# Opening of a hybrid attention and convolution layer: the first two blocks of products in another order, the first weight rows by two queues, two unread products fewer

## The chip, the cores and the metric

The kernel runs on one core of a Trainium2 chip. The metric is device time in microseconds (us) of one execution; lower is better. A core has five engines that run their own instruction lists side by side: TensorE (PE, matrix products; its weight loads are listed as PEld), VectorE (DVE), ScalarE (ACT), GpSimd (POOL) and SyncE (SP, which here only issues DMAs). They wait for one another by semaphores. DMAs are issued by SP, ACT and POOL.

## The reference, cut to what matters

One decoder layer on 512 tokens of width 2048:

```python
h = _rmsnorm(x, g_pre)
proj = h @ w_in                       # 2048 x 7168, all float32
q, k, v, z_att, u, g_glu, z_conv = jnp.split(proj, IN_SPLITS, axis=-1)
y_att  = stick_breaking_attention(q, k, v) * silu(z_att)
y_conv = conformer_conv(u, g_glu, ...) * silu(z_conv)   # starts with u * sigmoid(g_glu)
out = x + _rmsnorm(concat(y_att, y_conv) @ w_out, g_post)
```

The change touches only the start of `proj`: the first 512 columns of `g_glu`.

## The kernel before

Every float32 operand of a product is split into an upper part (`hi`, rounded to the format that PE takes) and a lower part (`lo`, the difference). A product of two such operands is three PE products that add up in one PSUM tile: upper by upper, upper by lower, lower by upper. One PE instruction multiplies a 128x128 tile by a 128x512 tile.

Nearly all of the kernel is a list of steps of such products, with the weights streamed in by DMA, split by ACT (`hi`) and DVE (`lo`), and used by PE. Ahead of the list stands the **opening**, which computes the first 512 columns of `g_glu` while `x` itself is still coming in. It works in 16 blocks: weight group `kg` of 0 to 3 (512 rows of `w_in`, tile `r_gn`, split into `h_gn` and `l_gn`) by token tile `m` of 0 to 3 (128 tokens). Four PSUM tiles `gn` (`ps0[m]`) collect the sums. The normalisation by the root of the mean square is multiplied in later, so the products can start on raw `x`.

For each block, `turn_block(n)` (L1255, by `turn_x`, L232) makes four 128x128 transposes of a tile of `x` on PE into a PSUM tile `xT`; then ACT writes the upper part into `h_hi` (L244) and DVE the lower part into `h_lo` (L245). For block 0 alone, DVE writes the upper part (L242) and, later, the lower part (`first_lo`, L247). `keep_raw` (L250) has ACT copy the raw transposed tile into `whole`. `rows_block` (L466) makes the products of a block: for each of four slices, `h_hi` by `h_gn` (L471) and `h_hi` by `l_gn` (L472), then four products of `h_lo` by `h_gn` (L478). The transposes of the next block are put in between: in block 0 after the third slice (`turn_at=2`), in the others after the first.

Group 0 of the weights comes as four tiles of 128 rows, 256 KB each (`load_w0_rows`, L1202), all issued by SP, between the first and the second tile of `x` (256 KB each as well). `part(0, i)` (L1211) splits row tile `i`: ACT writes `h_gn` (L102, multiplied by a column of `g_pre`), DVE `l_gn` (L103).

The order on PE, DVE and ACT in the opening is written out by hand, and each engine takes its instructions in the order of the program. Ahead of the first block, PE is kept at work by **unread products** (`idle_products`, L1242; tile `idle`): five before the transpose of `g_pre`, two after it, and four between the transposes of block 0 and its first product. Nobody reads their result. `plan` (L1271) hangs the rest of the work of ACT, DVE and the queues on the blocks: squares for the norm, splits of the next weights, further loads.

Of the kernel before, what the change touches and what calls it, by code (L numbers as in the profile page):

```python
# [16 lines left out]
P = 128  # L17
# [31 lines left out]
def hybrid_layer(  # L49
# [15 lines left out]
    nc = tc.nc  # L65
# [18 lines left out]
    def t2(name, dt=F32):  # L84
        return t2p.tile([P, S], dt, tag="t2", name=name)
# [4 lines left out]
    def mm(name):  # L90
        return mmp.tile([P, S], F32, tag="mm", name=name)

    def f32(ap):
        return ap.bitcast(F32)

    def split(hi, lo, src, scale=None):

        if scale is None:
            nc.scalar.activation(hi, src, AF.Copy)  # L99
            nc.vector.tensor_tensor(out=lo, in0=src, in1=f32(hi), op=ALU.subtract)  # L100
        else:
            nc.scalar.activation(hi, src, AF.Copy, scale=scale)  # L102
            nc.vector.scalar_tensor_tensor(  # L103
                out=lo, in0=src, scalar=scale, in1=f32(hi), op0=ALU.mult, op1=ALU.subtract
            )
# [123 lines left out]

    raw_h = {(m, 0): whole[:, :, m * P : (m + 1) * P] for m in range(NT)}  # L230

    def turn_x(m, j):  # L232

        ps = trp.tile([P, S], F32, tag="tr", name=f"xT{m}_{j}")
        for i in range(4):
            cs = slice(i * P, (i + 1) * P)
            nc.tensor.transpose(ps[:, cs], xts[m][j][:, cs], ident)
        src = ps.rearrange("p (i t) -> p i t", i=4)
        ms = slice(m * P, (m + 1) * P)
        hi, lo = h_hi[j][:, :, ms], h_lo[j][:, :, ms]  # L240
        if (m, j) == (0, 0):
            nc.vector.tensor_copy(hi, src)  # L242
        else:
            nc.scalar.activation(hi, src, AF.Copy)  # L244
            nc.vector.tensor_tensor(out=lo, in0=src, in1=f32(hi), op=ALU.subtract)  # L245

        def first_lo():  # L247
            nc.vector.tensor_tensor(out=lo, in0=src, in1=f32(hi), op=ALU.subtract)

        def keep_raw():  # L250
            if j > 0:
                raw_h[m, j] = t2(f"xw{m}_{j}").rearrange("p (i t) -> p i t", i=4)
            if (m, j) == (0, 0):
                first_lo()
            nc.scalar.copy(raw_h[m, j], src)

        return keep_raw
# [88 lines left out]
    def h_at(k, lo=0, hi=S):  # L346
        return h_hi[k // 4][:, k % 4, lo:hi], h_lo[k // 4][:, k % 4, lo:hi]
# [115 lines left out]
    def g_src(kg):  # L463
        return w_in[kg * S : (kg + 1) * S, C_G : C_G + S]

    def rows_block(kg, m, ps, w, between=(), turn_at=0):  # L466

        hi, lo = w
        parts = [h_at(kg * 4 + i, m * P, (m + 1) * P) for i in range(4)]
        for i, (a, _) in enumerate(parts):  # L470
            nc.tensor.matmul(ps, a, hi[:, i, :], start=kg + i == 0, stop=False, skip_group_check=True)  # L471
            nc.tensor.matmul(ps, a, lo[:, i, :], start=False, stop=False, skip_group_check=True)  # L472
            if i == turn_at:
                for f in between:
                    f()
        for i, (_, a) in enumerate(parts):
            last = kg == 3 and i == 3
            latest[0] = nc.tensor.matmul(  # L478
                ps, a, hi[:, i, :], start=False, stop=last, skip_group_check=True
            ).ins  # L480
# [33 lines left out]
    def sum_next(todo):  # L514

        if todo:
            tc.add_manual_dep(
                todo.popleft()().ins, latest[0].name,
                mybir.DependencyInfo(mybir.DependencyClass.Sync, mybir.DependencyReason.DATA),
                reason="not before its step",  # L520
            )
# [664 lines left out]
    ps0 = [mm(f"gn{m}") for m in range(NT)]  # L1186
    with tc.manual_schedule(engines={mybir.EngineType.DVE, mybir.EngineType.Activation}):
# [3 lines left out]
        w0 = {}  # L1191
# [10 lines left out]
        def load_w0_rows(i):  # L1202
            if 0 not in w0:
                w0[0] = (
                    raws.tile([P, 4, S], F32, tag="raw", name="r_gn0"),
                    his.tile([P, 4, S], F32R, tag="hi", name="h_gn0"),
                    los.tile([P, 4, S], F32R, tag="lo", name="l_gn0"),
                )
            nc.sync.dma_start(w0[0][0][:, i], g_src(0)[i * P : (i + 1) * P, :])

        def part(kg, i):  # L1211
            raw, hi, lo = w0[kg]
            k = kg * 4 + i
            split(hi[:, i], lo[:, i], raw[:, i], g_col[:, k : k + 1] if kg < 3 else None)
# [13 lines left out]
        for i in range(4):  # L1228
            load_w0_rows(i)
# [12 lines left out]
        def idle_products(count):  # L1242
            for i in range(count):
                nc.tensor.matmul(
                    idle.rearrange("p (n c) -> p n c", n=4), mean_w,
                    mean_w.unsqueeze(1).to_broadcast([P, 4, P]), start=True, stop=True,
                )
# [4 lines left out]
        blocks = [(kg, m) for kg in range(4) for m in range(NT)]  # L1252
        keeps = {}

        def turn_block(n):  # L1255
            kg, m = blocks[n]
            keeps[n] = turn_x(m, kg)
# [7 lines left out]
        def do(f, *args):  # L1265
            return partial(f, *args)
# [39 lines left out]
            15: [do(keep_rows, 2), do(next, first)],  # L1306
        }
        turn_block(0)
        idle_products(4)
        for i in range(4):  # L1310
            part(0, i)
        keeps[0]()
        for n, (kg, m) in enumerate(blocks):
            rows_block(
                kg, m, ps0[m], w0[kg][1:], [do(turn_block, n + 1)] if n + 1 < len(blocks) else (),
                2 if n == 0 else 0,
            )
            for f in plan[n]:
                f()
            if n + 1 < len(blocks):  # L1320
                keeps[n + 1]()
            if n >= 5 and n % 2:
                sum_next(v_sumq)
# [31 lines left out]
    for n, step in enumerate(steps):  # L1355
# [25 lines left out]
        w = loaded.pop(n)  # L1381
# [44 lines left out]
```

## Time and profile before

| | us |
|---|---|
| median of 3 runs | 860.49 |
| lowest to highest | 859.71 to 860.8 |
| profiled execution, device time | 860.66 |
| its span in the trace | 858.7 |
| PE busy in the span | 846.6 (99%) |

The span runs from the first to the last instruction that the trace shows; the remaining 1.96 us of the profiled execution lie around it. "Busy" of PE counts an instruction as busy from its start to its modelled end, waits of a product for its operand included; how fast PE moves is read from the distance between starts, which the chain of waits shows. In the chain, a row is a stretch that the next row had to wait for, or the instruction ahead of it on the same engine. Names in the rows leave out the buffer numbers: `gn` is any of the four PSUM tiles, `r_gn` any of the weight groups, `x` any of the 16 tiles of `x`.

### The profile page before, as it was taken

The page shows a single profiled execution, that of the slowest core. Times are in us where ns is not written, and L with a number is a line of the kernel's source. Part 1 is how long each engine was busy: PE and PEld are TensorE (multiplying, and loading weights), DVE is VectorE, ACT ScalarE, POOL GpSimd, SP SyncE. Part 2 cuts the span into 40 slices and gives each one's busy share as a digit, 9 for nine tenths or more (in the row PEclk, how much of TensorE's full clock was granted, in tenths as well). Part 3 has the DMA queues.
Part 4 walks back from the last instruction along what each step waited for, and adds up shares of the span by engine and source line. Part 5 has one row for each costly group of instructions (what it writes and reads, how often), then busy time and mean ns, then how long its engine had stood idle before and what let it go on. Part 6 is the DMA issues. An engine that isn't in the chain of part 4 may idle for free.

```text
span 858.7 us, 9932 instructions
## 1 busy us (share of the span) xinstructions
PE 846.6 (99%) x3868; PEld 701.9 (82%) x3868; DVE 660.7 (77%) x795; ACT 416.3 (48%) x473; POOL 139.4 (16%) x170
## 2 busy tenths in 40 slices
PE   9999999999999999999999999999999999999995
PEld 6888888788888888888888888888888888888884
DVE  5798899767579798897969898368964776468775
ACT  6784222555444342436432535369844355455542
POOL 0111110010130224222031334330000100000031
PEclk9999999999999999999999999999999999999999
DMA  8698989475877879867689887937755995557783
GB/s 322 236 291 186 326 262 248 151 239 196 295 224 227 244 147 207 283 181 208 190 221 187 239 244 152 289 103 289 295 196 196 222 267 196 197 197 269 281 279 100
DMA packets 92134, 195.04 MB, mean 227 GB/s; under 512 B 3686, under 2 KB 45938, under 8 KB 86712
## 3 DMA queue, kind: packets, MB, share of 16 engines
q1 hardware_dynamic: 66400, 120.61, 40.9%
q0 software_dynamic: 22304, 69.21, 33.8%
q10 hardware_dynamic: 3384, 4.59, 1.5%
q8 instruction: 30, 0.49, 0.2%
q14 instruction: 16, 0.13, 0.0%
HBM read 186.01 MB, written 75.50 MB: 305 GB/s over the span
## 4 chain that ended last, share of the span: by engine, by line
PE 84%; DVE 8%; DMA 4%; ACT 2%; issue 1%; POOL 0%; DVEq 0%; ACTq 0%; POOLq 0%
PE za L343 3%; PE za L342 3%; PE za L344 3%; PE a L1067 3%; PE a L1065 3%; PE a L1066 3%; PE u L344 3%; PE u L343 3%; PE u L342 3%; DVE acc L401 3%; PE q L344 3%; PE k L344 3%; PE q L342 3%; PE k L343 3%; PE k L342 3%; PE q L343 3%
## 5 line engine op out<-in xcount | busy, mean ns | idle before, releaser
L401 DVE SCALAR_TENSOR_TENSOR acc<-hg,vec,acc 128x512 f32<-128x512 f32 x240 | 181.4, 756 | 7.3
L100 DVE TENSOR_TENSOR l_w<-r_w,h_w 128x2048 fp32r<-128x2048 f32 x28 | 64.1, 2291 | 42.6 <-ACT h_w L99 42.6
L99 ACT ACTIVATE h_w<-r_w 128x2048 fp32r<-128x2048 f32 x28 | 53.6, 1915 | 44.4 <-DMA r_w<-ws 14.7
L342 PE MATMUL u<-h_hi,h_u 128*128 128x512 f32 x128 | 50.1, 391 | 0.0
L342 PE MATMUL q<-h_hi,h_q 128*128 128x512 f32 x128 | 50.1, 391 | 0.0
L342 PE MATMUL za<-h_hi,h_za 128*128 128x512 f32 x128 | 50.0, 391 | 0.0
L342 PE MATMUL k<-h_hi,h_k 128*128 128x512 f32 x128 | 50.0, 391 | 0.0
L344 PE MATMUL k<-h_hi,l_k 128*128 128x512 f32 x128 | 49.9, 390 | 0.0
L344 PE MATMUL u<-h_hi,l_u 128*128 128x512 f32 x128 | 49.9, 390 | 0.0
L344 PE MATMUL za<-h_hi,l_za 128*128 128x512 f32 x128 | 49.9, 390 | 0.0
L344 PE MATMUL q<-h_hi,l_q 128*128 128x512 f32 x128 | 49.9, 390 | 0.0
L343 PE MATMUL u<-h_lo,h_u 128*128 128x512 f32 x128 | 49.8, 389 | 0.0
L343 PE MATMUL k<-h_lo,h_k 128*128 128x512 f32 x128 | 49.8, 389 | 0.0
L343 PE MATMUL za<-h_lo,h_za 128*128 128x512 f32 x128 | 49.8, 389 | 0.0
L343 PE MATMUL q<-h_lo,h_q 128*128 128x512 f32 x128 | 49.8, 389 | 0.0
L1065 PE MATMUL a<-h_w,f_hi 128*128 128x512 f32 x128 | 49.8, 389 | 0.0
L1066 PE MATMUL a<-l_w,f_hi 128*128 128x512 f32 x128 | 49.8, 389 | 0.0
L1067 PE MATMUL a<-h_w,f_lo 128*128 128x512 f32 x128 | 49.8, 389 | 0.0
L100 DVE TENSOR_TENSOR l_v<-r_v,h_v 128x2048 fp32r<-128x2048 f32 x14 | 32.0, 2289 | 17.0 <-ACT h_v L99 17.0
L100 DVE TENSOR_TENSOR l_z<-r_z,h_z 128x2048 fp32r<-128x2048 f32 x14 | 32.0, 2288 | 16.2 <-ACT h_z L99 16.2
L674 POOL TENSOR_SCALAR_AFFINE_SELECT t<-t 128x128 f32<-128x128 f32 x64 | 35.2, 585 | 53.6 <-ACT t L710 29.5
L99 ACT ACTIVATE h_v<-r_v 128x2048 fp32r<-128x2048 f32 x14 | 26.8, 1916 | 29.4 <-PE g L343 13.2
(370 smaller groups left out, 2239.5 us busy)
## 6 DMA issues: line engine op xcount, KB each, us to landing
ws<-in_w_out_dram POOLq DMA_DIRECT2D x24, 1024.0 KB, 9.4
r_w<-ws SPq DMA_DIRECT2D x16, 1024.0 KB
vs<-in_w_in_dram POOLq DMA_DIRECT2D x12, 1024.0 KB, 11.8
zs<-in_w_in_dram POOLq DMA_DIRECT2D x12, 1024.0 KB, 9.4
r_w<-in_w_out_dram SPq DMA_DIRECT2D x12, 1024.0 KB
r_u<-in_w_in_dram SPq DMA_DIRECT2D x8, 1024.0 KB
r_q<-in_w_in_dram SPq DMA_DIRECT2D x8, 1024.0 KB
r_k<-in_w_in_dram SPq DMA_DIRECT2D x8, 1024.0 KB
```

The source lines that it names most:

```text
L99: nc.scalar.activation(hi, src, AF.Copy)
L100: nc.vector.tensor_tensor(out=lo, in0=src, in1=f32(hi), op=ALU.subtract)
L342: nc.tensor.matmul(ps, wh, ah, start=first, stop=False)
L343: nc.tensor.matmul(ps, wh, al, start=False, stop=False)
L344: latest[0] = nc.tensor.matmul(ps, wl, ah, start=False, stop=last).ins
L401: bgq.append(lambda j=j: nc.vector.scalar_tensor_tensor(out=acc, in0=hg[:, j : j + S], scalar=vec[:, ct, j : j + 1], in1=acc, op0=ALU.mult ...
L674: nc.gpsimd.affine_select(out=blk, in_=blk, compare_op=ALU.is_gt, fill=0.0, base=0, pattern=[[-1, P]], channel_multiplier=1,)
L1065: nc.tensor.matmul(ps, fh[:, kk, ts], hi[:, k, :], start=st, stop=False, skip_group_check=True)
L1066: nc.tensor.matmul(ps, fh[:, kk, ts], lo[:, k, :], start=False, stop=False, skip_group_check=True)
L1067: nc.tensor.matmul(ps, fl[:, kk, ts], hi[:, k, :], start=False, stop=en, skip_group_check=True)
```

## The change

Four things change, all in the opening.

- Row tiles 0 and 2 of weight group 0 are issued by ACT's queue, row tiles 1 and 3 by SP's.
- Two of the four unread products between the transposes of block 0 and its first product are gone.
- Blocks 0 and 1 are taken apart. PE makes the products of the upper part of block 0 (the transposes of block 1 now stand after the second slice), those of block 1 (the transposes of block 2 after the third slice), and then the four products of the lower part of block 0 and the four of block 1. From block 2 on nothing changes.
- `first_lo` is called ahead of the blocks and no longer by `keep_raw`, and both raw copies (`keeps[0]`, `keeps[1]`) come after the upper products of both blocks. On ACT, the upper parts of blocks 1 and 2 thus come ahead of the raw copies of blocks 0 and 1.

```diff
+        if (m, j) == (0, 0):
+            lower_part.append(first_lo)
...
-            if (m, j) == (0, 0):
-                first_lo()
             nc.scalar.copy(raw_h[m, j], src)
...
-    def rows_block(kg, m, ps, w, between=(), turn_at=0):
+    def rows_block(kg, m, ps, w, between=(), turn_at=0, uppers=True, lowers=True):
...
-            nc.sync.dma_start(w0[0][0][:, i], g_src(0)[i * P : (i + 1) * P, :])
+            eng = nc.sync if i % 2 else nc.scalar
+            eng.dma_start(w0[0][0][:, i], g_src(0)[i * P : (i + 1) * P, :])
...
-        idle_products(4)
+        idle_products(2)
         for i in range(4):
             part(0, i)
+        lower_part[0]()
+
+        rows_block(0, 0, ps0[0], w0[0][1:], [do(turn_block, 1)], 1, lowers=False)
+        rows_block(0, 1, ps0[1], w0[0][1:], [do(turn_block, 2)], 2, lowers=False)
         keeps[0]()
+        keeps[1]()
         for n, (kg, m) in enumerate(blocks):
-            rows_block(
-                kg, m, ps0[m], w0[kg][1:], [do(turn_block, n + 1)] if n + 1 < len(blocks) else (),
-                2 if n == 0 else 0,
-            )
+            between = [do(turn_block, n + 1)] if 2 <= n < len(blocks) - 1 else ()
+            rows_block(kg, m, ps0[m], w0[kg][1:], between, uppers=n >= 2)
             for f in plan[n]:
                 f()
-            if n + 1 < len(blocks):
+            if 2 <= n + 1 < len(blocks):
                 keeps[n + 1]()
```

On PE, from the transposes of block 1 (`xT1`) on, the order before was this; `gn0` and `gn1` are the sums of blocks 0 and 1, `h_hi0` and `h_lo0` the parts of `x`, `h_gn0` and `l_gn0` those of the weights:

```order
L237 MATMUL xT1_0_212<-ident_91,x1_0_104 128x128 x4
L471 MATMUL gn0_139<-h_gn0_148,h_hi0_116 128x512
L472 MATMUL gn0_139<-l_gn0_149,h_hi0_116 128x512
L478 MATMUL gn0_139<-h_gn0_148,h_lo0_120 128x512 x4
L471 MATMUL gn1_140<-h_gn0_148,h_hi0_116 128x512
L472 MATMUL gn1_140<-l_gn0_149,h_hi0_116 128x512
L237 MATMUL xT2_0_228<-ident_91,x2_0_108 128x128 x4
```

On PE, from the last upper product of block 0 (its transposes `xT1` now stand two slices ahead of this point) to the last lower product of block 1, the order now is this:

```order
L476 MATMUL gn0_139<-l_gn0_149,h_hi0_116 128x512
L475 MATMUL gn1_140<-h_gn0_148,h_hi0_116 128x512
L476 MATMUL gn1_140<-l_gn0_149,h_hi0_116 128x512
...
L239 MATMUL xT2_0_224<-ident_91,x2_0_108 128x128 x4
L475 MATMUL gn1_140<-h_gn0_148,h_hi0_116 128x512
L476 MATMUL gn1_140<-l_gn0_149,h_hi0_116 128x512
L482 MATMUL gn0_139<-h_gn0_148,h_lo0_120 128x512 x4
L482 MATMUL gn1_140<-h_gn0_148,h_lo0_120 128x512 x4
```

The eight products of lower parts moved behind all upper products of both blocks, and the transposes of block 2 with them from the first slice of block 1 to its third.

On ACT, from the splits of the weight rows on, the order before was this:

```order
L102 ACTIVATE h_gn0_148<-r_gn0_147,g_col_125 128x512 x4
L255 COPY whole_131<-xT0_0_186 128x4x128
L244 ACTIVATE h_hi0_116<-xT1_0_212 128x4x128
L255 COPY whole_131<-xT1_0_212 128x4x128
L244 ACTIVATE h_hi0_116<-xT2_0_228 128x4x128
```

On ACT, from the issue of the two row tiles on, it now is this:

```order
L1214 DMA r_gn0_147<-in_w_in_dram 128x512 x2
L102 ACTIVATE h_gn0_148<-r_gn0_147,g_col_125 128x512 x4
L246 ACTIVATE h_hi0_116<-xT1_0_207 128x4x128
L246 ACTIVATE h_hi0_116<-xT2_0_224 128x4x128
L258 COPY whole_131<-xT0_0_186 128x4x128
L258 COPY whole_131<-xT1_0_207 128x4x128
```

The two upper parts moved ahead of the two raw copies, and two DMA issues are new. The order on DVE is what it was; SP has two issues fewer and is otherwise the same.

## Rows read from the trace of the kernel before

**Rows 1.** The head of the page, and its busy time by engine (us, share of the span, instructions).

```profile
span 858.7 us, 9932 instructions
PE 846.6 (99%) x3868; PEld 701.9 (82%) x3868; DVE 660.7 (77%) x795; ACT 416.3 (48%) x473; POOL 139.4 (16%) x170
```

**Rows 2.** The chain of waits in order of time, from the start to the first product of block 2: start us, us, what.

```profile
1.77 2.50 PE idle L1244 x5
...
5.63 0.99 PE xT L237 x4
6.62 1.65 PE idle L1244 x4
8.27 0.23 PE gn L471
...
8.95 0.28 PE gn L472
...
9.46 0.42 PE gn L472
9.88 0.44 PE xT L237 x4
...
10.55 0.23 PE gn L472
10.79 1.06 PE gn L478 x4
11.85 0.47 PE gn L471
...
12.55 0.44 PE xT L237 x4
...
14.38 0.93 PE gn L478 x4
15.31 0.23 PE gn L471
```

**Rows 3.** The timeline of DVE in the same stretch, looked at in narrow windows (start us, us, what, in brackets the idle time before and who ended it); rows of "x2" hold two splits that overlap, of which the first starts at the time shown.

```profile
6.66 0.69 DVE L242 CAST h_hi<-xT 128x512 fp32r<-128x512 f32 x1 [1.97 <-PE xT L237]
7.26 0.74 DVE L103 SCALAR_TENSOR_TENSOR l_gn<-r_gn,g_col,h_gn 128x512 fp32r<-128x512 f32 x1
7.92 1.41 DVE L103 SCALAR_TENSOR_TENSOR l_gn<-r_gn,g_col,h_gn 128x512 fp32r<-128x512 f32 x2
9.25 0.74 DVE L103 SCALAR_TENSOR_TENSOR l_gn<-r_gn,g_col,h_gn 128x512 fp32r<-128x512 f32 x1
9.91 0.68 DVE L248 TENSOR_TENSOR h_lo<-xT,h_hi 128x512 fp32r<-128x512 f32 x1
```

**Rows 4.** The timeline of ACT: the first split of a weight row, the third and fourth, the first raw copy, the upper part of block 1, and the first split of weight group 1.

```profile
6.18 0.72 ACT L102 ACTIVATE h_gn<-r_gn,g_col 128x512 fp32r<-128x512 f32 x1 [4.10 <-DMA r_gn<-in_w_in_dram]
7.45 1.36 ACT L102 ACTIVATE h_gn<-r_gn,g_col 128x512 fp32r<-128x512 f32 x2
10.68 0.59 ACT L255 COPY whole<-xT 128x512 f32<-128x512 f32 x1 [1.88 <-DVE h_lo L248]
11.16 0.60 ACT L244 ACTIVATE h_hi<-xT 128x512 fp32r<-128x512 f32 x1
16.98 1.34 ACT L102 ACTIVATE h_gn<-r_gn,g_col 128x512 fp32r<-128x512 f32 x2
```

**Rows 5.** The timeline of the loads: the first and the last row tile as SP issues them (start us, us of the issue), PE's first transposes, which wait for the first tile of `x`, and the load that SP issues once the second tile of `x` has landed.

```profile
1.23 0.42 SPq L1209 DMA_DIRECT2D r_gn<-in_w_in_dram  x1
2.76 0.43 SPq L1209 DMA_DIRECT2D r_gn<-in_w_in_dram  x1
5.50 0.71 PEld L237 LDWEIGHTS xT<-ident,x 128*128 128x128 f32 x4 [0.60 <-DMA x<-in_x_dram]
8.68 0.33 SPq L141 DMA_DIRECT2D x<-in_x_dram  x1
```

**Rows 6.** The table by stretches of time: from:to us, length, busy us of each engine, then PEclk (granted clock), mean share of the DMA engines, GB/s.

```profile
3.00:4.00 1.00, 1.00 (x3) 0.46 (x2) 0.00 (x0) 0.00 (x0) 0.00 (x0) 1.00 0.76 115
6.00:7.00 1.00, 1.00 (x5) 0.90 (x5) 0.34 (x1) 0.81 (x2) 0.00 (x0) 1.00 1.04 399
```

**Rows 7.** The view of the DMA queues (packets, MB, share of the 16 DMA engines): first SP's queue (q1) at 11 to 14 us, where it works alone, then ACT's queue (q10) and SP's at 80 to 88 us, where both and POOL's are at work.

```profile
q1 hardware_dynamic: 613, 1.18, 103.7%
...
q10 hardware_dynamic: 428, 0.78, 25.5%
q1 hardware_dynamic: 460, 0.45, 21.1%
```

**Rows 8.** The view of waits from 12 to 850 us, for PE (the one row of that answer) and for its weight loads (the three longest): who waited for whom, us in total, times, longest.

```profile
PE va L638 <- DVE l_v L100: 1.2, 1, 1.2
...
PEld va L638 <- DVE l_v L100: 1.6, 1, 1.6
PEld vb L638 <- DVE l_v L100: 0.9, 2, 0.5
PEld gn L471 <- ACT h_hi L244: 0.4, 1, 0.4
```

**Rows 9.** Rows of the chain of waits and of POOL's timeline after the opening: the transposes that release the norm, a copy of weights that POOL issues when PE has read a buffer, a load of weights, the split that waits for it, and the split at which PE's longest wait ends.

```profile
41.03 0.45 PE r_ps L273 x4
...
60.58 0.50 POOL L506 DMA_DIRECT2D vs<-vs  x1 [5.42 <-PE gn L478]
...
92.96 20.43 DMA r_k<-in_w_in_dram
113.50 1.93 ACT h_k L99
154.78 2.30 DVE l_v L100
```

More of the change, by code (lines that the diff above doesn't have):

```diff
@@ L230, in hybrid_layer @@
     raw_h = {(m, 0): whole[:, :, m * P : (m + 1) * P] for m in range(NT)}
+    lower_part = []
     def turn_x(m, j):
@@ L464, in g_src @@
         return w_in[kg * S : (kg + 1) * S, C_G : C_G + S]
-    def rows_block(kg, m, ps, w, between=(), turn_at=0):
+    def rows_block(kg, m, ps, w, between=(), turn_at=0, uppers=True, lowers=True):
         hi, lo = w
         parts = [h_at(kg * 4 + i, m * P, (m + 1) * P) for i in range(4)]
-        for i, (a, _) in enumerate(parts):
+        for i, (a, _) in enumerate(parts if uppers else ()):
             nc.tensor.matmul(ps, a, hi[:, i, :], start=kg + i == 0, stop=False, skip_group_check=True)
@@ L475, in rows_block @@
                     f()
-        for i, (_, a) in enumerate(parts):
+        for i, (_, a) in enumerate(parts if lowers else ()):
             last = kg == 3 and i == 3
```

## The prediction, made before the change was run

> **What bounds the kernel now.** I read the page first: PE is busy in 99% of the span [rows 1]. Then I asked the view of waits where PE stands still after the opening: from 12 to 850 us there is one wait of PE itself, 1.2 us on `l_v`, and its weight loads show hardly more than that same one again [rows 8]. So from about 12 us on PE runs nearly without a gap to the end, and an earlier end of the opening is worth its full length, if whatever feeds PE moves with it. That sends the reader to the first 16 us of the chain of waits [rows 2]. A product of 128x512 takes 0.23 us of the chain there once things run, and four transposes 0.44. From the first real product (8.27) to the first of block 2 (15.31) lie 7.04 us. In them stand 24 products, 24 x 0.231 = 5.54, and two sets of transposes, 0.88: 6.42. The other 0.62 us are waits: 0.05 and 0.19 where `l_gn` is late (the rows of 0.28 and 0.42), 0.13 at the first lower product (1.06 for four where block 1 needs 0.93), and 0.24 at the first product of block 1 (0.47). What is late is seen in DVE: from the end of PE's transposes it works through a chain, `h_hi` at 6.66, four `l_gn` 0.66 apart, then `first_lo` to 10.59 [rows 3]. ACT's raw copy of block 0 waits 1.88 us for that `first_lo`, and the upper part of block 1 stands behind the copy on ACT [rows 4]. Ahead of 8.27, PE is only filled by unread products.
>
> **The order of the products.** I lay the new order over the old times of DVE, whose list is unchanged. The transposes of block 0 end at 6.62. Two unread products at 1.65/4 = 0.41 each end at 7.45, not 8.27 [rows 2]. `h_hi` is there at 6.66 + 0.69 = 7.35, the first `h_gn` at 6.18 + 0.72 = 6.90 [rows 3, 4], so the first product runs 7.45 to 7.86, still at the price of the unread ones. The second needs the first `l_gn`: 7.26 + 0.74 = 8.00, so with 0.05 for the hand-over it runs from 8.05 to 8.28; the third to 8.51; the fourth needs the second `l_gn`, 7.92 + 0.74 = 8.66, and ends at 8.95. The transposes of block 1 need the second tile of `x`. It had landed by 8.68 before, since SP then issued the load that waited for it [rows 5]; they end at 9.39. Four more products, with the third and fourth `l_gn` at 9.33 and 9.99 [rows 3], end at 10.31. Block 1 needs its upper part from ACT, which has been done with the splits since 7.45 + 1.36 = 8.81: 9.39 + 0.60 + hand-over = 10.05, in time. Six products (1.39), transposes (0.44), two products (0.46) end at 12.60. The lower parts are ready by 10.59 and about 11.3 on DVE, and eight products at 0.232 end at 14.46, where block 2 begins; before, 15.31. The **gain is 0.85 us**: PE starts 0.82 earlier, pays 0.18 more for a first product at the early price, and waits 0.41 instead of 0.62.
>
> **What ACT moves.** The raw copies come two upper parts later on ACT, about 12.8 and 13.3 where they were 10.68 and 12.5; only the norm far behind reads them. The squares and the copy of block 2 follow, and ACT has some 3 us there: its next fixed date is the split of weight group 1 at 16.98 [rows 4], set by a 1 MB load, and block 4 uses it at 15.31 + 6.42 = 21.7 before, 20.9 now. If that cover were gone, PE would wait for ACT at block 4, by at most the 0.85 won.
>
> **Two queues.** Rows 0 and 2 on ACT's queue cost ACT two issues of about 0.42 [rows 5], in the 4.10 us in which it waits for the first row [rows 4]: free. SP has 2 x 0.47 less to issue, and its later loads then wait on partly other landings; the 1 MB load of weight group 1 may be issued some 0.6 later, behind several loads still in flight: free. What do rows gain by it? SP issued the four between 1.23 and 2.76, yet ACT's splits were 0.63 apart as they came [rows 4, 5], and the engines moved 399 GB/s at 6 to 7 us: 256 KB in 0.66 us [rows 6]. The rows come at the pace of the transfer, not of the issue. And an earlier row buys nothing: DVE's chain starts with `h_hi`, set by the first tile of `x` at 5.50 [rows 3, 5]. So the gain of this part is zero, and its risk is that first tile: it had the engines to itself, and now row 0 runs beside it. That queues do take from one another shows at 80 to 88 us, where SP's queue moved 0.45 MB in 8 us, against 1.18 MB in 3 us alone [rows 7]. The delay lies between 0 (at 3 to 4 us the engines moved only 115 GB/s [rows 6], there is room) and 0.66 us, a whole row tile put in front; less than 0 is excluded, as nothing is taken out from ahead of that tile. I take 0.3: the rows of both ends are equally near. DVE's chain, and with it all that I laid out, moves by this.
>
> The Trainium skill ("DMA: Bandwidth & Descriptors", section "Issuing engines are not separate DMA queues") says that loads from different engines run on the same DMA engines and interleave, and that issuing from several saves only the time of the issue. Rows 5 to 7 agree; by that rule alone the second queue gives nothing here and the interleaving is its only effect.
>
> **Sum.** 0.85 - 0.30 = 0.55 us. What comes after moves along: the transposes that release the norm stand on PE at 41.03, the copies of weights are issued when PE has read a buffer (60.58, after 5.42 us of waiting), and the load that took 20.43 us at 92.96 and set ACT's split at 113.50 stands in that traffic [rows 9]. From the profiled execution, 860.66 - 0.55 = 860.11 us (858.15 of span and 1.96 around it); the median of the runs is 0.17 below it. I predict **859.9 us** as median. The forecast's own range, for a delay of 0.66 to 0 and 0.3 of run to run, is 859.3 to 860.6.
>
> **Rival: the clock rises later (slower).** The windows name a granted clock of 1.00 everywhere [rows 6], but the durations don't agree: unread products took 0.41 to 0.50 until 8.27, and the same shape 0.23 from there [rows 2], as 512 columns do at 1.2 and at 2.4 GHz (0.43 and 0.21). So PE ran at the lower level until about 8.2 us, and before the rise it was filled from 6.62 on without a hole and before that by transposes. Now it stands still from 7.86 to 8.05, and between the unread products and the transposes if the tile of `x` is late. If the rise slips, every product costs 0.20 more and a set of transposes 0.99 instead of 0.44 [rows 2]. At the lower level, with 0.43 a product, the upper products of block 0 after 8.05 (seven, and one set of transposes) would end at 12.05, not 10.31; as PE is then the late one, a late tile of `x` no longer adds. Block 2 would start at 16.20, 0.89 later than before: 861.4. It decides from about 10.3 us: if PE is still at 1.2 GHz then, the gain is gone.
>
> The Trainium skill ("TensorE: Matmul & The Clock Gate", section "What's actually happening") says that the lower clock is the default and that activity lifts it, which speaks against taking filling away. The rows fit that, but no run here has taken any away.
>
> **Rival: the gain is swallowed.** PE's wait of 1.2 us for `l_v` ends with a split at 154.78, and the chain to it passes a load of 20.43 us in crowded traffic [rows 8, 9]. If that landing doesn't move, PE waits there the longer: 860.5. For it speaks the length of the load; against it that its traffic is set off by PE.
>
> **Rival: more than the sum.** If the first tile of `x` is not late, 0.85; if the wait on `l_v` also falls away, up to 1.2 more: 858.4 to 859.6. Nothing in the rows says why it should fall away.
>
> **Chances.** The forecast 0.53; the clock later 0.25; swallowed 0.13; more than the sum 0.09. The range of 8 in 10 reaches over the forecast, the swallowed case and the clock's case to its price: 859.0 to 861.4. Faster or slower means by over 0.2% (1.72 us), about what a measurement of this kernel can tell from no change. Faster needs the last rival nearly in full: 0.07. Slower needs a clock that stays low into block 1: 0.06. The same: 0.87.
>
> **What would show it.** Right: in the chain, the first product of block 2 near 14.8 instead of 15.31, the first real product near 7.5 to 8, no long first products in blocks 0 and 1, `first_lo` ending at 10.6 to 11.2, and PE's later waits as before. Wrong: products of 0.43 after 8.3 (clock); transposes of block 0 at 6 us or later (two queues); rows that land earlier and a chain of DVE that starts before 6.66; or the wait on `l_v` longer by what the opening won.

## The result, and the profile after

The changed kernel took **862.19 us** as the median of 22 runs (861.11 to 869.03), the kernel before 860.79 as the median of 22 on the same chip (859.34 to 865.62). The ratio is 1.0027 [1.0014, 1.004]: slower, since the whole interval lies above 1. The medians lie 1.40 us apart, the means 2.0, and the ratio stands for 2.3: 5 of the 22 runs of the changed kernel took 866 us or more, none of the kernel before did, and such runs move a mean but hardly a median. The prediction was 859.9, in a range that ended at 861.4.

The profiled run took 861.86 us. Its page begins like this, against [rows 1]:

```profile
span 859.9 us, 9927 instructions
PE 847.9 (99%) x3866; PEld 703.1 (82%) x3866; DVE 661.1 (77%) x795; ACT 416.2 (48%) x473; POOL 139.4 (16%) x170
```

PE has two instructions fewer and is busy 1.3 us longer, so some of the same products take longer. The chain of waits to block 2 shows where (start us, us, what; against [rows 2]):

```profile
1.49 6.05 DMA r_gn<-in_w_in_dram
...
8.40 0.80 PE gn L475
9.19 0.79 PE gn L476
9.98 0.43 PE gn L475
...
13.39 0.43 PE gn L475
13.82 0.27 PE gn L476
14.09 0.23 PE gn L475
...
15.91 1.83 PE gn L482 x8
17.75 0.23 PE gn L475
```

Two things are to be seen. First, the chain begins with row 0: ACT issues it at 1.49, and its split cannot start before 7.62, where it started at 6.18 [rows 4]. Second, products stay at 0.43 us until 13.82, and come at 0.23 only from 14.09; before, they ran at 0.23 from 8.27. Block 2 begins at 17.75 instead of 15.31, 2.44 later.

The timeline shows what stood in the way: ACT, DVE and PE of the same stretch (start us, us, what, in brackets the idle time before and who ended it).

```profile
7.62 1.34 ACT L102 ACTIVATE h_gn<-r_gn,g_col 128x512 fp32r<-128x512 f32 x2 [5.54 <-DMA r_gn<-in_w_in_dram]
...
8.38 2.93 DVE L103 SCALAR_TENSOR_TENSOR l_gn<-r_gn,g_col,h_gn 128x512 fp32r<-128x512 f32 x4 [0.64 <-ACT h_gn L102]
...
5.90 1.12 PE L239 MATMUL xT<-ident,x 128*128 128x128 f32 x4 [0.27 <-DMA x<-in_x_dram]
6.66 1.20 PE L1249 MATMUL idle<-mean_w 128*128 128x512 f32 x2
8.40 0.80 PE L475 MATMUL gn<-h_gn,h_hi 128*128 128x512 f32 x1 [0.53 <-ACT h_gn L102]
```

The transposes of block 0 start 0.40 later than before (5.90 against 5.50 [rows 5]). DVE's chain of `l_gn` starts at 8.38, not 7.26 [rows 3], and now it is row 0 that it waits for. PE stands still for 0.53 before its first real product. The queues (packets, MB, share of the DMA engines) tell why row 0 is late. First the changed kernel at 3 to 5 us, then the same at 5 to 7 us, then SP's queue in the kernel before at 5 to 7 us, where it works alone:

```profile
q1 hardware_dynamic: 161, 0.29, 55.8%
q10 hardware_dynamic: 42, 0.07, 11.5%
...
q10 hardware_dynamic: 205, 0.38, 49.3%
q1 hardware_dynamic: 219, 0.40, 53.8%
...
q1 hardware_dynamic: 427, 0.78, 102.7%
```

Two things delay row 0, a tile of 0.26 MB. ACT's queue (q10) moved only 0.07 MB at 3 to 5 us, although ACT issued the row at 1.49. From 5 us on it and SP's queue (q1) moved nearly the same number of bytes, together what SP's queue moved alone before: SP's later rows and tiles of `x` got half of the traffic just when the chain needed row 0.

Behind the opening, 1.2 of the 2.44 us are missing in the span. PE's wait for `l_v` is 0.3 here, against 1.2 before [rows 8]; this is the whole answer for PE from 12 to 850 us:

```profile
PE va L642 <- DVE l_v L100: 0.3, 1, 0.3
```

Whether the later opening shortened that wait, or whether it differs from one execution to another, two traces cannot say; the experiments come back to it.

### The profile page after: what moved, and what is told of

It is laid out like the page before. It is cut to its first block, busy times and chain, and to the rows that moved or that the text cites. A ratio compares the mean times of both kernels' runs of the same rounds, so it can differ in the third digit from the quotient of the medians.

```text
span 859.9 us, 9927 instructions
## 1 busy us (share of the span) xinstructions
PE 847.9 (99%) x3866; PEld 703.1 (82%) x3866; DVE 661.1 (77%) x795; ACT 416.2 (48%) x473; POOL 139.4 (16%) x170
## 4 chain that ended last, share of the span: by engine, by line
PE 85%; DVE 7%; DMA 4%; ACT 2%; issue 1%; DVEq 0%; ACTq 0%
PE za L346 3%; PE za L345 3%; PE za L347 3%; PE a L1069 3%; PE a L1070 3%; PE a L1071 3%; PE u L347 3%; PE u L346 3%; PE u L345 3%; DVE acc L404 3%; PE q L347 3%; PE k L347 3%; PE q L345 3%; PE k L346 3%; PE k L345 3%; PE q L346 3%
```

## The experiments

**Theory A**: the second queue is the cause; it delays row 0, and PE's hole keeps the clock at the lower level. **Theory B**: two unread products fewer are enough for the clock to rise late. Further letters stand for the theories that each expectation weighs. "Opening" is the start of block 2's first product in the one profiled run; "not timed" is a kernel of which there is that run alone.

| kernel | opening, us | profiled run, us | median (runs), us | before, same chip | ratio |
|---|---|---|---|---|---|
| before | 15.31 | 860.66 | | | |
| after | 17.75 | 861.86 | 862.19 (22) | 860.79 | 1.0027 [1.0014, 1.004] |
| order_only | 14.80 | 859.29 | 859.52 (11) | 859.93 | 0.9995 [0.9983, 1.0008] |
| order_idle | 14.70 | 859.47 | 859.80 (11) | 859.93 | 0.9999 [0.9981, 1.0017] |
| queues_only | 16.54 | 861.47 | 862.94 (12) | 859.93 | 1.0043 [1.0024, 1.0062] |
| idle_only | 15.26 | 859.65 | 860.09 (11) | 859.93 | 0.9997 [0.9981, 1.0013] |
| after_idle6 | 16.22 | 864.90 | not timed | 860.06 | |
| rows_all_act | 19.00 | 864.09 | not timed | 860.06 | |
| rows_swapped | 14.85 | 861.35 | not timed | 860.06 | |
| delay_only | 15.93 | 861.53 | 861.50 (11) | 860.06 | 1.0017 [1.0008, 1.0026] |
| delay_big | 17.92 | 863.01 | 863.00 (7) | 860.53 | 1.003 [1.0019, 1.0042] |
| after_idle6_timed | 16.77 | 863.32 | 861.17 (11) | 860.53 | 1.0001 [0.9983, 1.0019] |
| order_hi_first | 14.82 | 859.70 | 859.70 (11) | 860.53 | 0.9989 [0.9974, 1.0003] |
| order_only_again | 14.82 | 860.68 | 859.45 (11) | 859.63 | 0.9991 [0.9979, 1.0003] |

**The three parts, each alone.** First the new order with every row on SP's queue and four unread products:

```diff
-            eng = nc.sync if i % 2 else nc.scalar
-            eng.dma_start(w0[0][0][:, i], g_src(0)[i * P : (i + 1) * P, :])
+            nc.sync.dma_start(w0[0][0][:, i], g_src(0)[i * P : (i + 1) * P, :])
...
-        idle_products(2)
+        idle_products(4)
```

> Only the new order of products and raw copies; all rows by SP, four unread products. Theory A (the second queue is the loss: it brings row 0 of the weights later): the first product of block 2 comes at about 14.7 us instead of 15.31, 860.2 us against 860.8 before. Theory B (fewer unread products are the loss, by a later rise of the clock): the same, since none is taken away here. Rival C (the order itself loses): 861 to 862.

The same with two unread products, as the change has them:

```diff
-            eng = nc.sync if i % 2 else nc.scalar
-            eng.dma_start(w0[0][0][:, i], g_src(0)[i * P : (i + 1) * P, :])
+            nc.sync.dma_start(w0[0][0][:, i], g_src(0)[i * P : (i + 1) * P, :])
```

> New order and two unread products fewer, all rows by SP. Theory A: first product of block 2 at about 14.5 us, 860.0 us. Theory B: products of 0.43 us after 8.3 us of the span, first product of block 2 at 16 us or later, 861 to 861.7 us.

The kernel before with the two queues alone:

```diff
-            nc.sync.dma_start(w0[0][0][:, i], g_src(0)[i * P : (i + 1) * P, :])
+            eng = nc.sync if i % 2 else nc.scalar
+            eng.dma_start(w0[0][0][:, i], g_src(0)[i * P : (i + 1) * P, :])
```

> Only rows 0 and 2 by ACT's queue; old order, four unread products. Theory A: row 0 splits on ACT near 7.6 us instead of 6.18, DVE's chain 1.2 us later, first product of block 2 near 16.5 us, 861.3 to 862 us. Theory B: rows as before, 860.8 us.

And the kernel before with two unread products fewer alone:

```diff
-        idle_products(4)
+        idle_products(2)
```

> Only two unread products fewer; old order, all rows by SP. Theory A: first product of block 2 at 15.3 us, because the upper part of block 1 still waits on ACT behind the raw copy; 860.8 us. Theory B: products of 0.43 us after 8.3 us, first product of block 2 at 16 us or later, 861.5 us.

The opening ended at 14.80 with the order alone, 14.70 with the order and fewer unread products, 15.26 with fewer unread products alone, and 16.54 with the queues alone. Of order_idle, without the second queue, PE's two unread products in the timeline, and then the chain:

```profile
6.24 0.94 PE L1248 MATMUL idle<-mean_w 128*128 128x512 f32 x2
...
8.04 0.50 PE gn L476
...
8.77 0.43 PE gn L476
...
12.89 1.81 PE gn L482 x8
14.70 0.23 PE gn L475
```

The chain of queues_only, with all four unread products in place:

```profile
7.01 1.71 PE idle L1245 x4
...
9.22 0.79 PE gn L472
10.01 0.43 PE gn L471
10.44 0.24 PE gn L472
...
16.54 0.23 PE gn L471
```

Theory B fell: with two unread products fewer, the clock had long risen when the eight lower products took 1.81, which is 0.23 each, and neither order_idle nor idle_only is slower than the kernel before. Theory A stands: the second queue alone costs 1.23 us of opening, by late data and by products that take 0.43 and more until 10.44. But the parts do not add up: order -0.51, queues +1.23 and unread products -0.05 make 0.67, and the changed kernel lost 2.44. Two unread products fewer open the hole of 0.53 only when row 0 is late; order_idle waits 0.28 there, for `h_hi`. The median of queues_only is 3.0 above the kernel before, more than the opening can account for: 5 of its 12 runs took 864 us or more (see the last section).

**How much is the clock, how much the late row?** The changed kernel with PE's hole filled by six unread products:

```diff
-        idle_products(2)
+        idle_products(6)
```

> The changed kernel with six unread products where it has two, so that PE is filled until row 0 of the weights is split. Theory A1 (row 0 comes late by the second queue, and the low clock is a consequence of the hole that PE then has): row 0 still splits near 7.6 us, but the products after about 9 us take 0.23 us, and the first product of block 2 comes near 16 us instead of 17.75. Theory A2 (the low clock comes with the order or by chance): products of 0.43 us again, block 2 near 17.7 us.

ACT's first split came at 7.62 again, so the loads were as in the changed kernel. The chain:

```profile
6.90 2.56 PE idle L1249 x6
9.46 0.43 PE gn L475
...
10.21 0.23 PE gn L475
...
16.22 0.23 PE gn L475
```

With the hole filled, products run at 0.23 from 10.21, not from 14.09, and block 2 begins 1.53 earlier than in the changed kernel, although PE did four products more. That is what the clock cost in this pair of traces. What is left against order_idle, 16.22 - 14.70 = 1.52, is put down to the late rows: DVE's last `l_gn` ends 1.34 later here than there (11.31 against 9.97). Some of the 1.52 may be the filling itself, which ends at 9.46, while the split of row 0 was done at about 8.3. The run itself took 864.90, which the opening does not explain: PE waited later for weights. The view of waits from 12 to 850 us, and the load in the chain behind it:

```profile
PE q L347 <- DVE l_q L100: 1.6, 1, 1.6
...
PE k L347 <- DVE l_k L100: 1.0, 1, 1.0
...
72.64 21.66 DMA r_q<-in_w_in_dram
```

So the same kernel was timed:

> The changed kernel with six unread products where it has two, timed. Its first product of block 2 came at 16.22 us, 1.5 us earlier than in the changed kernel, with the loads as there. Theory P: 0.7 to 1.5 us less than the changed kernel, 861 us. Theory Q: the median falls as little as 0.3 us, since runs at 865 us stay.

(The edit is the same.) The opening of this profile ended at 16.77, so the clock's part is 1.0 to 1.5 us between the two. The median was 861.17, ratio 1.0001 [0.9983, 1.0019]: filling the hole takes most of the loss away, though this interval and that of the changed kernel, 1.0014 to 1.004, still overlap a little.

**What two queues do to the rows.** All four rows on ACT's queue:

```diff
-            eng = nc.sync if i % 2 else nc.scalar
+            eng = nc.scalar
```

> The changed kernel with all four rows on ACT's queue; SP has only tiles of x. Theory S (while both queues hold work each gets half of the transfer): rows 0 to 3 are split about 1.3 us apart, the last near 11.5 us, while the second tile of x has landed by 7.5 us instead of 9.5. Rival (ACT's queue only starts late and then runs at full rate): the first row near 7.6 us, the others 0.65 us apart.

The timeline of ACT from 5 us on, its last two issues and the splits that wait for the rows (the releaser in brackets is the row's load):

```profile
4.96 0.91 ACTq L1214 DMA_DIRECT2D r_gn<-in_w_in_dram  x2
6.84 0.72 ACT L102 ACTIVATE h_gn<-r_gn,g_col 128x512 fp32r<-128x512 f32 x1 [4.75 <-DMA r_gn<-in_w_in_dram]
8.22 0.72 ACT L102 ACTIVATE h_gn<-r_gn,g_col 128x512 fp32r<-128x512 f32 x1 [0.66 <-DMA r_gn<-in_w_in_dram]
...
11.26 0.72 ACT L102 ACTIVATE h_gn<-r_gn,g_col 128x512 fp32r<-128x512 f32 x1 [0.31 <-DMA r_gn<-in_w_in_dram]
```

The first two rows are 1.38 us apart and all four 1.47 on average ((11.26 - 6.84) / 3), where one queue alone brought one in about 0.67 (0.78 MB in 2 us): with SP's tiles of `x` on the other queue, they come at less than half the pace. The expected spacing was 1.3. The rival's full rate behind a late start did not come; the late start did (ACT's queue moved 0.10 MB at 3 to 5 us, SP's 0.36). For the third and fourth row this is not the sharing alone, since ACT's queue took their issues only at 4.96. In its chain the clock did something that nobody expected:

```profile
11.43 0.43 PE gn L475
...
15.74 0.43 PE gn L476
...
19.00 0.23 PE gn L475
```

Products took 0.43 until after 15.74, later than in any other kernel; the last section has what stood ahead of them.

The two queues the other way round, rows 1 and 3 on ACT's:

```diff
-            eng = nc.sync if i % 2 else nc.scalar
+            eng = nc.scalar if i % 2 else nc.sync
```

> The changed kernel with rows 1 and 3 on ACT's queue and rows 0 and 2 on SP's. Theory S: row 0, now right behind the first tile of x on SP's queue, splits near 6.9 us, row 1 near 7.6; DVE's chain starts near 7.7 and block 2 about 0.7 us earlier than in the changed kernel at the same clock. Rival (any second queue delays the first row to 7.6): no difference.

Row 0, on SP's queue again, is split at 6.59, and the opening ends at 14.85, as with one queue, so the rival fell: in this trace two queues leave the opening early, as long as row 0 is not on the second one. Block 2 came 2.90 earlier than in the changed kernel, not 0.7, since products ran at 0.23 from about 8.6. But the profiled run took 861.35. The timeline of ACT and the weight loads' waits from 12 to 40 us:

```profile
18.78 1.34 ACT L102 ACTIVATE h_gn<-r_gn,g_col 128x512 fp32r<-128x512 f32 x2 [2.11 <-DMA r_gn<-in_w_in_dram]
...
PEld gn L475 <- ACT h_hi L246: 0.7, 1, 0.7
```

The split of weight group 1 started 1.80 later than the 16.98 of before [rows 4], and `h_hi` of a later block, behind it on ACT, held PE's weight loads for 0.7. What the opening won was lost at block 4. This is one run of a kernel that was not timed, and its end cannot be told from the spread of runs.

**Does a later opening reach the end?** The kernel before with 14, then with 22 unread products in place of 4; the second diff differs in that number alone:

```diff
-        idle_products(4)
+        idle_products(14)
```

> The kernel before with fourteen unread products where it has four: the opening is made later on PE, and no DMA is touched. First product of block 2 near 17 us instead of 15.31. Theory D (an opening that ends 1 to 2 us later costs the end about half of that, the rest is taken out of PE's later waits): 860.6 to 861.2 us against about 860. Theory E (all of it passes): 861.5 to 862. Theory F (the kernel's cost comes from the DMAs' new order and not from PE's delay): 860.

> The kernel before with 22 unread products where it has four: first product of block 2 near 17.7 us, as late as in the changed kernel, but every load comes as before. Theory P (a late opening is the whole cost, however it came about): about the time of the changed kernel, 2 us over the kernel before, 862 us, and now and then a run at 865 us or more, as the changed kernel has in 5 of its 22 runs. Theory Q (the runs at 865 us or more come from the loads being in another order): 861.5 to 862.5 us and no run over 864 more often than before.

The openings ended at 15.93 and 17.92, that is 0.62 and 2.61 later. The medians rose by 1.44 (by the ratio's interval 0.7 to 2.2) and 2.47 (1.6 to 3.6). The opening of delay_only was expected near 17. Its chain shows why it came earlier:

```profile
6.28 3.21 PE idle L1244 x14
```

The fourteen unread products took 0.23 each from 6.28 on. In the kernel before, whose list on PE is the same up to there, they took 0.41 until 8.27 [rows 2]. So the clock rises up to 2 us earlier or later in executions of the same work, and how much of the 13.82 in the one trace of the changed kernel is chance cannot be read from that trace.

The longer delay arrives in full, and PE still waited 1.1 for `l_v` in it, so a late opening does not by itself shorten that wait. The shorter arrives with more than its length; why is open.

**Is there more in the order?** The version order_idle, with block 0's first four products all of the upper weight part, so that `l_gn` is needed later:

```diff
+        if kg == 0 and m == 0 and uppers:
+            for i, (a, _) in enumerate(parts):
+                nc.tensor.matmul(ps, a, hi[:, i, :], start=i == 0, stop=False, skip_group_check=True)
+            for f in between:
+                f()
+            for i, (a, _) in enumerate(parts):
+                nc.tensor.matmul(ps, a, lo[:, i, :], start=False, stop=False, skip_group_check=True)
+            uppers = False
```

> New order, two unread products, all rows by SP, and in block 0 the four products with the upper parts of the weights first, then the transposes of block 1, then the four with the lower parts, so that PE waits for DVE's chain once and not at each row. First product of block 2 near 14.1 us against 14.7 and 15.31. If the end follows the opening: 859 us against 860; if PE's later waits swallow it: 859.8.

> The kernel with the new order alone once more, to see whether it beats the kernel before. Its opening ended 0.5 us earlier. If an earlier opening reaches the end in full, 0.5 us less than before (a ratio of 0.9994); if PE's later waits swallow it, no difference. Neither theory expects a run to lie 2 us over the kernel before.

(The second repeats order_only.) The opening of order_hi_first ended at 14.82 and not at 14.1. Its chain:

```profile
6.10 2.65 ACT h_gn L102 x4
...
8.79 0.50 PE gn L476
9.29 0.44 PE xT L239 x4
9.73 0.94 PE gn L480 x4
```

The four products with `l_gn` (L480) run at 0.23 each without a wait. In their place the fourth product with `h_gn` (L476) waits, for ACT's split of row 3, which ends at 8.75: the new order exchanges a wait for DVE's chain for one on ACT's splits. The medians of the versions with one queue were below the kernel before by 0.41 and 0.18 (order_only, twice), 0.13 (order_idle) and 0.83 (order_hi_first), and each interval reaches past 1: a version that beats both kernels was not shown. All of them beat the changed kernel, by opening and median. The two runs of order_only also show what one profile is worth at the end: 859.29 and 860.68, with waits of 0.7 and 1.2 for `l_v`. The 0.3 in the profile after is thus no proof of anything that the change did.

## Why the prediction was wrong, step by step

- **What bounds the kernel**: right. A pure delay of 2.61 came through as 2.47; one of 0.62 came through as more than itself.
- **The order of the products**: right in mechanism and sign, too large. It said 0.85; order_idle won 0.61 and order_only 0.51 of the opening. The difference of order_idle to the laid-out end, 14.70 against 14.46, arises at the second product: laid out from 8.05 to 8.28, it took from 8.04 to 8.53, 0.50 instead of 0.23 behind its wait for `l_gn`. From there on the layout held within 0.05. That waits on the splits and not PE's own work set this part shows again in order_hi_first, where the wait is for ACT.
- **What ACT moves**: free, as said, in the changed kernel and with one queue. The cover that I named, the split of weight group 1, was gone in rows_swapped: 2.11 of idle time on ACT, and PE waited 0.7, below the bound of 0.85.
- **Two queues**: this is the step that failed. It priced the first tile of `x` and nothing else ("its risk is that first tile"). The tile was 0.40 late, inside 0 to 0.66 and near the 0.3 taken. But row 0 itself was split 1.44 later, and the text had ruled that out as a matter of gain: "an earlier row buys nothing", since DVE's chain starts with `h_hi`. A *later* row was not asked about. Before, `l_gn` started at 7.26 behind `h_hi`, on a row split at 6.18 to 6.90, so there was 0.36 of slack; 1.44 went through it. That the rows come at the pace of the transfer was true (0.78 MB in 2 us), though the 0.63 between ACT's splits is no proof of it: two splits whose data have landed follow one another as closely (1.34 for two of 0.72 [rows 4]). If the pace is the transfer's, a row that shares the engines half and half with tiles of `x` loses pace to them. The queue view before showed such sharing [rows 7], and I applied it to the tile alone. That ACT's queue would also move only 0.07 MB at 3 to 5 us, no row of the kernel before showed. The late rows cost about 1.5 us of opening (16.22 against 14.70). Nor was the load of weight group 1 as free as said: SP issued it at 9.49 instead of 8.07, 1.42 later and not 0.6. In the changed kernel PE was later still, but in rows_swapped it waited.
- **The clock as a rival**: the mechanism was right and its size too small. It gave 0.89 slower, with products of 0.43 up to 12.05; they lasted until 13.82. The cause that the rival named, a hole of 0.19 before the second product, was not tested: in order_idle PE waits 0.28 for `h_hi` at 7.47, but its two unread products took 0.94 against 1.20 in the changed kernel, so the clock had risen ahead of that hole. The holes that the second queue made are 0.27 before the transposes and 0.53 before the first product. The first alone does not keep the clock down until 13.8: queues_only has it too, and its products ran at 0.23 from 10.44. With the second one filled, they did so from 10.21 and 10.97, and the ratio came back to 1.0001. So the hole of 0.53, with the waits behind it, is the likely cause, by one trace with it and three without, and by the times. The test that I gave, "if PE is still at 1.2 GHz" at 10.3, told the cases apart rightly. The clock's part is 1.0 to 1.5 us, from these traces.
- **The sum**: the 2.44 of the opening split into 0.61 won (order_idle), 1.52 lost by late rows (after_idle6 against it) and 1.53 by the clock (after against after_idle6). These are differences along one row of traces and add up by construction; with the trace of after_idle6_timed, the last two are 2.07 and 0.98. The medians are only 1.40 apart. The profile of after has 0.9 less waiting for `l_v`, but that wait ranges from 0.3 to 1.2 over kernels without any pattern by opening. That the medians show less than the opening is open; the ratio's own interval, 1.2 to 3.4 us, reaches over the whole 2.44.

The Trainium skill ("DMA: Bandwidth & Descriptors", section "Issuing engines are not separate DMA queues") says that loads interleave whichever engine started them, and that issuing from several saves the time of the issue only. The runs agree: 0.40 and 0.38 MB side by side in 2 us, 0.78 MB before, and no row earlier. The cost here lies in whose bytes went beside the critical ones.

## What to carry to other kernels

The second queue for loads that the transfer limits brought none of them earlier here; it handed half of the traffic to what used to stand behind. With row 0 left on the first queue, the same two queues kept the early opening (14.85), though that one run was still long (861.35). Before splitting such loads, write down for each one, not only the one that the chain waits for now, how much later it may land before its consumer becomes the late one. And a hole that late data leaves in PE while the clock is still to rise may cost as much as the data: fill it until the data are sure to be there.

## What the runs showed of the hardware

**Sharing is by queue, about half and half.** Over 5 to 7 us the two queues moved 0.40 and 0.38 MB, where SP's alone had moved 0.78 MB, and with four rows on ACT's queue, 0.87 and 0.73 MB over 6 to 10 us:

```profile
q1 hardware_dynamic: 471, 0.87, 57.2%
q10 hardware_dynamic: 401, 0.73, 48.2%
```

**ACT's queue starts late.** Sharing alone does not give the 1.44 of row 0. In all five kernels with rows on ACT's queue that queue moved 0.06 to 0.11 MB over 3 to 5 us, and SP's 0.28 to 0.36. In the changed kernel ACT issued its first row at 1.49, only 0.26 behind SP's first row, so the issue does not explain it; why the queue starts so late is open. Nor is the end of row 0 settled. ACT's queue moved 0.38 MB within 5 to 7 us, more than row 0's 0.26 MB, yet row 0 was complete only at 7.54: part of that traffic was row 2, while a last piece of row 0 was still out. In rows_all_act row 0 was split at 6.84, earlier, on the same queue.

**The lower clock comes back.** In rows_all_act PE's timeline shows the two unread products and the first real one so:

```profile
6.09 0.71 PE L1249 MATMUL idle<-mean_w 128*128 128x512 f32 x2
...
7.62 0.50 PE L475 MATMUL gn<-h_gn,h_hi 128*128 128x512 f32 x1 [0.82 <-ACT h_gn L102]
```

The two took 0.71 there, against 1.20 in the same view of the changed kernel: the clock had risen. PE then waited 0.82 and twice 0.28, and the table by stretches (columns as in [rows 6]) shows the granted clock fall within 9 to 10 us:

```profile
9.00:10.00 1.00, 0.72 (x2) 0.40 (x2) 0.73 (x1) 0.00 (x0) 0.00 (x0) 0.73 1.06 393
10.00:11.00 1.00, 1.00 (x4) 0.82 (x5) 0.02 (x1) 0.72 (x1) 0.00 (x0) 0.50 1.01 387
```

It stayed at 0.50, the lower level, up to 16 us, and products took 0.43 from 11.43 to after 15.74. The Trainium skill ("TensorE: Matmul & The Clock Gate", section "What's actually happening") has the lower clock as the default that activity lifts. The traces agree: each begins with five unread products in 2.50 us, 0.50 each, and reaches 0.23 later.

**More long runs with two queues.** Of the kernels with a second queue in the opening 13 of 48 runs took 864 us or more; of those with the loads as before, 10 of 182, and none of the 18 with a delayed opening alone. One trace of such a run, after_idle6, shows a load of 21.66 us at 72.64 and PE waiting 2.6 for its weights behind it. Such a load alone is not the cause: one of 20.43 us stands in the chain of the kernel before [rows 9] and one of 22.11 in that of order_idle, whose profiled runs were short. Why loads 70 us later should feel the opening's queues is not settled.
